# A feed-forward up projection with both halves of the split tokens in one 512-column matmul, and a gate through Silu

## The chip, the cores and the metric

The kernel runs on one core of one Trainium2 chip. The metric is the device time of one execution in microseconds (us), and the kernel before takes 456.35 us (median of 3 runs, 455.64 to 457.35).

## The reference

One layer of a transformer trunk on 256 tokens of width 1024: a sparse-attention mixer, a cross attention to 256 memory tokens, and a convolutional feed-forward block, each behind an RMS norm and added to the residual, with a last RMS norm. Everything is float32. The change sits in the feed-forward block:

```python
def conv_ffn(h, w_up, conv_w, w_down):          # w_up 1024 x 5632, w_down 2816 x 1024
    gate, val = jnp.split(h @ w_up, 2, axis=-1)
    return (jax.nn.silu(causal_dwconv(gate, conv_w)) * val) @ w_down
```

`causal_dwconv` is a causal convolution over the tokens with three taps per channel.

## The kernel before

TensorE multiplies in the type fp32r. To keep float32 accuracy every operand is split into a high part (the value copied to fp32r by ScalarE, `split_hi`, L200, or L122 for weights) and a low part (value minus high part, a subtraction on VectorE, `split_lo`, L204, or L126 for weights). A product is then three matmuls into the same accumulator, `mm3` (L195 to L197): high weight by high token, high weight by low token, low weight by high token. The product of the two low parts is left out.

Weights stream from HBM in half chunks of 128 x 1024 (`load_half`, L114, on SP's queue). Each half is split ahead of its use: ScalarE writes `hi` (L122), VectorE writes `lo` (L126), into six buffers each, so that a split can start only when the matmuls that read the sixth half before it are done. `half` (L129) runs this some four halves ahead of the matmul that asks for the weight (`wtile`, L152).

The feed-forward block works on 22 tiles of 128 gate channels and 128 value channels (`NF`, index `fi`). Its tokens are `h3`, transposed, eight blocks of 128 channels by 256 tokens, high and low part in a tile each. The first three tiles (`ups`, L1095 to L1105) are computed with the tokens as the stationary operand, half of the tokens at a time, copied by ScalarE (`ut`) and transposed back on TensorE into two banks of the tag S and one of O; they start before the second half of the tokens is normed. The other 19 tiles go through `proj_ws` (L290): the weights are stationary, the 256 tokens move, eight steps of three matmuls for the gate (left half of a PSUM bank) and eight for the value (right half). Their banks rotate over the tags PT, proj and S, two banks each.

Behind each tile, ScalarE copies the gate to SBUF (`g`, L1116) and scales it by the last tap (`c`, L1119), VectorE adds the other two taps (L1120, L1121), ScalarE takes the tanh of half the sum (L1123), VectorE forms the gate (L1124) and multiplies it by the value, which it reads from PSUM (`av`, L1126). ScalarE and VectorE then split `av` into `aT_hi` (L200) and `aT_lo` (L204). The down projection (`pd`, L1144 to L1153) reads these, with tokens stationary and 512 or 256 weight columns moving.

SP's and GpSimd's instructions keep the order in which they are written (`manual_schedule`). For TensorE, ScalarE and VectorE a planner fixes the order of the feed-forward block when the program is built, by its own estimate of when operands and buffers are ready. On the chip each engine then runs its list in that order and waits where an operand is late.

Of the kernel before, what the change touches and what calls it, by code (L numbers as in the profile page):

```python
# [10 lines left out]
F32 = mybir.dt.float32  # L11
F32R = mybir.dt.float32r
BF16 = mybir.dt.bfloat16
AF = mybir.ActivationFunctionType
ALU = mybir.AluOpType
AX = mybir.AxisListType

P = 128
D = 1024
S = 256  # L20
NT = S // P
KT = D // P
# [20 lines left out]
def trunk_kernel(ctx: ExitStack, tc: tile.TileContext, a, out):  # L43
    nc = tc.nc
# [4 lines left out]
    act = ctx.enter_context(tc.tile_pool(name="act", bufs=1))  # L49
# [3 lines left out]
    def bank(tag, name):  # L53
        return psum.tile([P, 512], F32, tag=tag, name=name, bufs=2)
# [26 lines left out]
    def add_chunks(name, n, width=2048, start=0):  # L81
        first = len(chunks)
        for i in range(start, start + n):
            chunks.append((a[name][i], width))
        return first
# [66 lines left out]
    def wtile(i, k, c, n):  # L152

        hi, lo = half(i, k // 4, k % 4)
        o = (k % 4) * 256 + c
        return hi[:, o:o + n], lo[:, o:o + n]
# [28 lines left out]
    c_up = add_chunks("w_up", NF)  # L185
# [6 lines left out]
    def mm3(ps, lw, rx, start, stop):  # L192

        (lh, ll), (rh, rl) = lw, rx
        nc.tensor.matmul(ps, lh, rh, start=start, stop=False)  # L195
        nc.tensor.matmul(ps, lh, rl, start=False, stop=False)  # L196
        nc.tensor.matmul(ps, ll, rh, start=False, stop=stop)  # L197
# [85 lines left out]
    def act_pair(nm, tag, pool=act):  # L283
        return tuple(pool.tile([P, KT, S], F32R, tag=f"{tag}_{x}", name=f"{nm}_{x}") for x in ("hi", "lo"))

    def xk(pair, k, t=None):
        s = slice(0, S) if t is None else slice(t * P, (t + 1) * P)
        return pair[0][:, k, s], pair[1][:, k, s]

    def proj_ws(ps, ci, ct, pair, t=None):  # L290

        for k in range(KT):
            mm3(ps, wtile(ci, k, ct * P, P), xk(pair, k, t), k == 0, k == KT - 1)

    def proj_ws_steps(ps, ci, ct, pair):

        for k in range(KT):
            mm3(ps, wtile(ci, k, ct * P, P), xk(pair, k), k == 0, k == KT - 1)
            yield
# [41 lines left out]
    with tc.tile_pool(name="attn", bufs=1, reuse_waits="tile") as at:  # L341
# [9 lines left out]

        hT = act_pair("hT", "aA")

        xT = act.tile([P, KT, S], F32, tag="aB_hi", name="xT")
        rs_x = at.tile([P, NT], F32, name="rs_x")


# [2 lines left out]
        with tc.manual_schedule():  # L360
# [32 lines left out]
            for k0, k1 in PIECES:  # L393
# [3 lines left out]
                if not o:  # L397
                    his.setdefault(c_v + h // 2, []).append(
                        wpool.tile([P, NHALF], F32R, tag="hi", name=f"hi{c_v + h // 2}_{h % 2}", bufs=NBUF))
                    lo = wpool.tile([P, NHALF], F32R, tag="lo", name=f"lo{c_v + h // 2}_{h % 2}", bufs=NBUF)  # L400
                    parts.setdefault(c_v + h // 2, []).append((his[c_v + h // 2][h % 2], lo))
                hi, lo = parts[c_v + h // 2][h % 2]
                cs = slice(o * 512, (o + k1 - k0) * 512)
                split((hi[:, cs], lo[:, cs], v_raw[h][:, cs]))
                for w in range(2):
                    for t in range(NT):
                        for k in ks:
                            rx = (hi, lo)[w][:, (k % 2) * 512:(k % 2 + 1) * 512]
                            for x in range(2 - w):
                                nc.tensor.matmul(pv[t], xk(hT, k, t)[x], rx, start=k == 0 and w == x == 0,  # L410
                                                 stop=k == KT - 1 and w == 1)
# [274 lines left out]
        rs_m = mp.tile([P, NT], F32, name="rs_m")  # L686
        with tc.tile_pool(name="aq", bufs=1, reuse_waits="tile") as aq:

            memT = act_pair("memT", "aB")

            def mem_keys(ci):
                def out(c, ps):
# [303 lines left out]
    with tc.tile_pool(name="cross", bufs=1, reuse_waits="tile") as cr:  # L996
# [46 lines left out]
        def cross_o(h, pT):  # L1043
            po = bank("O", f"xo{h}")
            for dt in range(2):
                col = h * S + dt * P
                for c in range(2):
                    nc.tensor.matmul(po[:, dt * S:(dt + 1) * S], MV[:, c, col:col + P], pT[:, c, :],
                                     start=c == 0, stop=c == 1)
            ks = slice(2 * h, 2 * h + 2)  # L1050
            split((oX[0][:, ks, :], oX[1][:, ks, :], po.rearrange("p (c s) -> p c s", c=2)))
# [6 lines left out]
        for t in range(NT):  # L1058
            for ci in range(EARLY):
                ps = bank("proj", f"pcq{t}{ci}")  # L1060
# [10 lines left out]
        for h in range(4):  # L1071
# [4 lines left out]
                    tick()  # L1076
                tick()
            cross_o(h, pT)
        h3 = act_pair("h3", "aB")
        residual(c_wo, oX, "wo",  # L1080
                 lambda t, sums: norm_t(x_sb[:, t, :], t, h3, C_FFN, f"ffn{t}", "PT", sums),
                 0)
# [4 lines left out]
    with tc.tile_pool(name="ffn", bufs=1, reuse_waits="tile") as fp:  # L1087
        aT = (fp.tile([P, NF, S], F32R, name="aT_hi2"), fp.tile([P, NF, S], F32R, name="aT_lo2"))
        NG = 3
        gbuf = [fp.tile([P, S + 2], F32, name=f"g{i}") for i in range(NG)]  # L1090
        for gb in gbuf:
            nc.gpsimd.memset(gb[:, 0:2], 0.0)

        FIRST = 3
        ups = {fi: bank(("S", "S", "O")[fi], f"up{fi}") for fi in range(FIRST)}  # L1095
        for t in range(NT):
            for fi in range(FIRST):
                ps = bank("proj", f"upt{t}{fi}")
                for k in range(KT):
                    mm3(ps[:, :S], xk(h3, k, t), wtile(c_up + fi, k, 0, S), k == 0, k == KT - 1)  # L1100
                ut = fp.tile([P, S], F32, tag="ut", name=f"ut{t}{fi}", bufs=2)
                nc.scalar.activation(ut, ps[:, :S], AF.Copy)
                for gv_ in range(2):
                    o = gv_ * S + t * P
                    nc.tensor.transpose(ups[fi][:, o:o + P], ut[:, gv_ * P:(gv_ + 1) * P], ident)  # L1105
        wfin = fp.tile([P, D], F32, name="wfin")
        nc.scalar.dma_start(wfin, a["final_w"].to_broadcast([P, D]))
        for fi in range(NF):
            if fi in ups:
                ps = ups.pop(fi)  # L1110
            else:
                ps = bank(("PT", "proj", "S")[fi % 3], f"up{fi}")
                for gv_ in range(2):
                    proj_ws(ps[:, gv_ * S:(gv_ + 1) * S], c_up + fi, gv_, h3)
            gb = gbuf[fi % NG]
            nc.scalar.activation(gb[:, 2:], ps[:, :S], AF.Copy)  # L1116
            c = fp.tile([P, S], F32, tag="c", name=f"c{fi}", bufs=2)
            cw = [cc[:, C_CONV + j * NF + fi:C_CONV + j * NF + fi + 1] for j in range(3)]
            nc.scalar.activation(c, ps[:, :S], AF.Copy, scale=cw[2])  # L1119
            nc.vector.scalar_tensor_tensor(c, gb[:, 1:S + 1], cw[1], c, op0=ALU.mult, op1=ALU.add)  # L1120
            nc.vector.scalar_tensor_tensor(c, gb[:, 0:S], cw[0], c, op0=ALU.mult, op1=ALU.add)  # L1121
            th = fp.tile([P, S], F32, tag="th", name=f"th{fi}", bufs=2)
            nc.scalar.activation(th, c, AF.Tanh, scale=0.5)  # L1123
            nc.vector.scalar_tensor_tensor(c, th, 1.0, c, op0=ALU.add, op1=ALU.mult)  # L1124
            av = fp.tile([P, S], F32, tag="av", name=f"av{fi}", bufs=2)
            nc.vector.scalar_tensor_tensor(av, c, 0.5, ps[:, S:2 * S], op0=ALU.mult, op1=ALU.mult)  # L1126
            split((aT[0][:, fi, :], aT[1][:, fi, :], av))


        H = D // 2  # L1130
        LAST = 6
        ssq = {t: [] for t in range(NT)}
        xw = fp.tile([P, D], F32, name="xw")
        y = [fp.tile([P, D], F32, name=f"y{t}") for t in range(NT)]

        def add_pd(pd, t, h, c0, c1):

            cs = slice(h * H + c0, h * H + c1)
            xs = x_sb[:, t, cs]
            nc.vector.tensor_tensor(xs, pd, xs, op=ALU.add)  # L1140
            ssq[t].append(sumsq(xs, f"f{t}{h}proj"))
            return cs

        for h in range(2):  # L1144

            accs = [(0, 0, H), (1, 0, H)] if h == 0 else [(0, 0, H), (1, 0, H // 2), (1, H // 2, H)]
            pd = [bank((("O", "PT"), ("proj", "proj", "S"))[h][n], f"pd{h}{n}") for n in range(len(accs))]
            plan = [(k, n) for k in range(NF - LAST) for n in range(len(accs))]
            plan += [(k, n) for n in range(len(accs)) for k in range(NF - LAST, NF)]
            for k, n in plan:  # L1150
                t, c, e = accs[n]
                w = wrow(c_dn[h] + k // 4, k % 4)
                mm3(pd[n][:, :e - c], xk(aT, k, t), (w[0][:, c:e], w[1][:, c:e]), k == 0, k == NF - 1)  # L1153
            for n, (t, c, e) in enumerate(accs):
                cs = add_pd(pd[n][:, :e - c], t, h, c, e)
                if t == 1 and n < 2:
                    nc.gpsimd.tensor_tensor(xw[:, cs], x_sb[:, 1, cs], wfin[:, cs], op=ALU.mult)
                elif t == 0 and h == 1:
                    rs = rstd(partial(ssq[0][:1], "f0"), ssq[0][1], "f0")
                    nc.vector.scalar_tensor_tensor(y[0], x_sb[:, 0], rs, wfin, op0=ALU.mult, op1=ALU.mult)  # L1160
                    nc.sync.dma_start(out[0:P, :], y[0])
        t1 = partial(ssq[1][:2], "f1")
        rs = rstd(t1, ssq[1][2], "f1")
        c = 768
        nc.vector.tensor_scalar(y[1][:, :H], xw[:, :H], rs, None, op0=ALU.mult)
        nc.sync.dma_start(out[P:, :H], y[1][:, :H])
        nc.scalar.activation(y[1][:, H:c], xw[:, H:c], AF.Copy, scale=rs)
        nc.vector.scalar_tensor_tensor(y[1][:, c:], x_sb[:, 1, c:], rs, wfin[:, c:], op0=ALU.mult, op1=ALU.mult)
        nc.scalar.dma_start(out[P:, H:], y[1][:, H:])
# [93 lines left out]
```

## Time and profile before

| | |
|---|---|
| median of 3 runs | 456.35 us |
| the profiled execution's own time | 456.24 us |
| its span, first to last instruction | 454.5 us |
| TensorE busy | 443.6 us (98%), 3274 matmuls |
| VectorE busy | 305.6 us (67%) |
| ScalarE busy | 278.8 us (61%) |

The up projection's own matmuls start at 273.4 us of the span, and the down projection takes over at 386.35 us. A busy time here is a union: an instruction whose start lies before the end of the one ahead of it adds only what sticks out. A matmul's listed duration is its time through the array and not what a stream of them pays for each, so costs of matmuls are read from start to start.

### The profile page before, as it was taken

Reading aid. Unit: us, or ns where it says so; the run is one execution under the profiler, and the core shown is the slowest. Engines: PE = TensorE matmul, PEld = TensorE weight load, DVE = VectorE, ACT = ScalarE, POOL = GpSimd, SP = SyncE. Lnnn points to the kernel's source line nnn. Section 1 sums busy time; section 2 is a strip of 40 time slices with the busy share of each in tenths; the row PEclk is TensorE's granted clock in tenths of the full one; section 3 lists DMA queues with packets and bytes.
Section 4 is the critical chain, followed back from the end, with each engine's and each line's share of the span. In section 5 each row is a group of like instructions: output and inputs, shape, how many; then the busy total and the mean of one; then the engine's idle time right before and its main releaser. Section 6 shows DMA issues by size and latency. Waiting matters only on the chain.

```text
span 454.5 us, 8504 instructions
## 1 busy us (share of the span) xinstructions
PE 443.6 (98%) x3274; PEld 406.9 (90%) x3274; DVE 305.6 (67%) x592; ACT 278.8 (61%) x569; POOL 38.7 (9%) x80
## 2 busy tenths in 40 slices
PE   8999999999999999999999999999999999999994
PEld 4999889899988778999988899999999999888984
DVE  4765489779776895756543858878777777745413
ACT  6785496768786886765552757666655556435301
POOL 4240000521200000100000010000000000001003
PEclk9999999999999999999999999999999999999999
DMA  8995958723232005554334537655555555554302
GB/s 295 370 376 186 315 211 273 220 95 112 94 94 94 1 1 191 180 182 147 118 107 143 179 104 238 222 187 187 184 187 184 184 185 183 186 191 154 127 0 94
DMA packets 22073, 77.04 MB, mean 170 GB/s; under 512 B 2576, under 2 KB 3088, under 8 KB 22032
## 3 DMA queue, kind: packets, MB, share of 16 engines
q1 hardware_dynamic: 21312, 74.39, 48.5%
q10 hardware_dynamic: 720, 2.10, 1.2%
q8 instruction: 26, 0.43, 0.4%
q14 instruction: 15, 0.12, 0.1%
HBM read 75.43 MB, written 1.05 MB: 168 GB/s over the span
## 4 chain that ended last, share of the span: by engine, by line
PE 84%; ACT 5%; DMA 4%; DVE 2%; issue 2%; POOL 1%; SPq 0%; POOLq 0%; DVEq 0%; ACTq 0%
PE up L195 8%; PE up L197 8%; PE up L196 8%; PE pd L196 5%; PE pd L197 5%; PE pd L195 5%; PE pt L852 2%; PE O L876 2%; PE pmk L197 2%; PE pmk L195 2%; PE pcq L195 2%; PE pmk L196 2%; PE pcq L196 2%; PE pmv L196 2%; PE pmv L195 2%; PE pmv L197 2%
## 5 line engine op out<-in xcount | busy, mean ns | idle before, releaser
L126 DVE TENSOR_TENSOR lo<-raw,hi 128x1024 fp32r<-128x1024 f32 x122 | 148.7, 1223 | 69.5 <-ACT hi L122 68.7
L122 ACT ACTIVATE hi<-raw 128x1024 fp32r<-128x1024 f32 x122 | 128.6, 1059 | 59.3 <-PE pd L197 17.7
L195 PE MATMUL up<-h_hi,hi 128*128 128x256 f32 x304 | 86.1, 283 | 0.0
L196 PE MATMUL up<-h_lo,hi 128*128 128x256 f32 x304 | 86.0, 283 | 0.0
L197 PE MATMUL up<-h_hi,lo 128*128 128x256 f32 x304 | 86.0, 283 | 0.0
L196 PEld LDWEIGHTS up<-h_lo,hi 128*128 128x128 f32 x304 | 58.4, 192 | 0.0
L197 PEld LDWEIGHTS up<-h_hi,lo 128*128 128x128 f32 x304 | 58.4, 192 | 0.0
L195 PEld LDWEIGHTS up<-h_hi,hi 128*128 128x128 f32 x304 | 58.4, 192 | 0.0
L197 PE MATMUL pd<-hi,aT_lo 128*128 128x512 f32 (+1 forms) x110 | 38.4, 349 | 0.0
L196 PE MATMUL pd<-lo,aT_hi 128*128 128x512 f32 (+1 forms) x110 | 38.4, 349 | 0.0
L195 PE MATMUL pd<-hi,aT_hi 128*128 128x512 f32 (+1 forms) x110 | 38.4, 349 | 0.0
L828 ACT ACTIVATE pp<-pp,nm 128x128 f32<-128x128 f32 (+1 forms) x64 | 28.4, 446 | 7.6 <-DVE nm L821 7.6
L821 DVE CUSTOM_DVE_ANT_0 pp<-s,tri,nrs 128x128 f32<-128x128 f32 (+1 forms) x64 | 23.4, 412 | 6.5 <-PE s L809 4.1
L196 PEld LDWEIGHTS pd<-lo,aT_hi 128*128 128x128 f32 x110 | 20.7, 188 | 2.9
L195 PEld LDWEIGHTS pd<-hi,aT_hi 128*128 128x128 f32 x110 | 20.7, 188 | 2.9
L197 PEld LDWEIGHTS pd<-hi,aT_lo 128*128 128x128 f32 x110 | 20.7, 188 | 2.9
L1123 ACT ACTIVATE th<-c 128x256 f32<-128x256 f32 x22 | 9.1, 414 | 22.2 <-DVE c L1121 22.2
L195 PE MATMUL pq<-hT_hi,hi 128*128 128x256 f32 x64 | 18.5, 289 | 0.4 <-ACT hi L122 0.4
L196 PE MATMUL pmv<-lo,memT_hi 128*128 128x256 f32 x64 | 18.5, 289 | 0.0
L195 PE MATMUL pmv<-hi,memT_hi 128*128 128x256 f32 x64 | 18.5, 288 | 0.0
L197 PE MATMUL pmk<-memT_hi,lo 128*128 128x256 f32 x64 | 18.3, 286 | 0.0
L197 PE MATMUL pq<-hT_hi,lo 128*128 128x256 f32 x64 | 18.3, 288 | 0.0
(295 smaller groups left out, 1096.5 us busy)
## 6 DMA issues: line engine op xcount, KB each, us to landing
raw<-in_w_up SPq DMA_DIRECT2D x44, 512.0 KB, 4.3
raw<-in_w_dn SPq DMA_DIRECT2D x20, 512.0 KB, 4.6
raw<-in_w_q SPq DMA_DIRECT2D x8, 512.0 KB, 6.1
raw<-in_w_mk SPq DMA_DIRECT2D x8, 512.0 KB, 5.0
raw<-in_w_mv SPq DMA_DIRECT2D x8, 512.0 KB, 4.0
raw<-in_w_out SPq DMA_DIRECT2D x8, 512.0 KB, 3.8
raw<-in_ca_wq SPq DMA_DIRECT2D x8, 512.0 KB, 4.3
raw<-in_ca_wo SPq DMA_DIRECT2D x8, 512.0 KB, 4.2
```

Source lines behind the costliest of these rows:

```text
L122: nc.scalar.activation(his[i][h], raws[i][h], AF.Copy)
L126: nc.vector.tensor_tensor(t, raws[i][h], f(his[i][h]), op=ALU.subtract)
L195: nc.tensor.matmul(ps, lh, rh, start=start, stop=False)
L196: nc.tensor.matmul(ps, lh, rl, start=False, stop=False)
L197: nc.tensor.matmul(ps, ll, rh, start=False, stop=stop)
L821: nc.vector.tensor_tensor_reduce(self.p[br], self.s[:, br * w:(br + 1) * w], tri[:, 1 - t:].rearrange("p h k -> p (h k)"), nrs[:, t:t + 1] ...
L828: nc.scalar.activation(self.p[br], self.p[br], AF.Exp, bias=pair.nm[:, j, br:br + 1], scale=-1.0, accum_out=pair.den[:, j, br:br + 1])
L852: nc.tensor.transpose(self.pt[n][:, o * P:(o + 1) * P], self.pp[:, j, br, h * P:(h + 1) * P], ident)
L876: nc.tensor.matmul(O[j * DK:(j + 1) * DK, pair.m * P:(pair.m + 1) * P], V[:, h, br, g, :], pair.block(j, br, h), start=False, stop=(br, h) ...
L1123: nc.scalar.activation(th, c, AF.Tanh, scale=0.5)
```

## The change

A new `act_both` puts the high and the low part of the tokens into one tile, for each block of channels 256 high columns and then 256 low ones. A new `proj_wide` replaces `proj_ws` for the 19 tiles: for each step the high weight meets all 512 columns in one matmul into a whole bank, and the low weight meets the 256 high columns, added into the left half of that bank. So the bank holds two sums that have still to be added, and the gate and the value have a bank each. The banks rotate over four tags, PT with proj for even tiles and S with O for odd ones.

On the way out ScalarE copies the left half to SBUF and VectorE adds the right half, for the gate into `g` and for the value into a new tile `vb`. The scaling by the last tap reads `g` instead of PSUM. Silu takes the place of the tanh and of the instruction that formed the gate from it, for all 22 tiles. The tile that held the transposed input and the memory's tokens ahead of `h3` takes the new shape too.

```diff
+    def act_both(nm):
+        both = act.tile([P, 2 * KT, S], F32R, tag="aB", name=nm).rearrange("p (k b) s -> p k b s", b=2)
+        return (both[:, :, 0], both[:, :, 1]), both
+
+    def proj_wide(ps, ci, ct, both):
+        for k in range(KT):
+            hi, lo = wtile(ci, k, ct * P, P)
+            nc.tensor.matmul(ps, hi, both[:, k], start=k == 0, stop=False, skip_group_check=True)
+            nc.tensor.matmul(ps[:, :S], lo, both[:, k, 0], start=False, stop=k == KT - 1, skip_group_check=True)
...
-        xT = act.tile([P, KT, S], F32, tag="aB_hi", name="xT")
+        xT = act.tile([P, 2 * KT, S], F32, tag="aB", name="xT")[:, :KT]
...
-            memT = act_pair("memT", "aB")
+            memT, _ = act_both("memT")
...
-        h3 = act_pair("h3", "aB")
+        h3, x3 = act_both("h3")
...
             if fi in ups:
                 ps = ups.pop(fi)
             else:
-                ps = bank(("PT", "proj", "S")[fi % 3], f"up{fi}")
+                wide = [bank(("PT", "proj", "S", "O")[(2 * fi + gv_) % 4], f"up{fi}{gv_}") for gv_ in range(2)]
                 for gv_ in range(2):
-                    proj_ws(ps[:, gv_ * S:(gv_ + 1) * S], c_up + fi, gv_, h3)
+                    proj_wide(wide[gv_], c_up + fi, gv_, x3)
+                ps = None
             gb = gbuf[fi % NG]
-            nc.scalar.activation(gb[:, 2:], ps[:, :S], AF.Copy)
             c = fp.tile([P, S], F32, tag="c", name=f"c{fi}", bufs=2)
             cw = [cc[:, C_CONV + j * NF + fi:C_CONV + j * NF + fi + 1] for j in range(3)]
-            nc.scalar.activation(c, ps[:, :S], AF.Copy, scale=cw[2])
+            if ps is None:
+                nc.scalar.activation(gb[:, 2:], wide[0][:, :S], AF.Copy)
+                nc.vector.tensor_tensor(gb[:, 2:], wide[0][:, S:], gb[:, 2:], op=ALU.add)
+                vb = fp.tile([P, S], F32, tag="vb", name=f"vb{fi}", bufs=2)
+                nc.scalar.activation(vb, wide[1][:, :S], AF.Copy)
+                nc.vector.tensor_tensor(vb, wide[1][:, S:], vb, op=ALU.add)
+            else:
+                nc.scalar.activation(gb[:, 2:], ps[:, :S], AF.Copy)
+                vb = ps[:, S:2 * S]
+            nc.scalar.activation(c, gb[:, 2:], AF.Copy, scale=cw[2])
             nc.vector.scalar_tensor_tensor(c, gb[:, 1:S + 1], cw[1], c, op0=ALU.mult, op1=ALU.add)
             nc.vector.scalar_tensor_tensor(c, gb[:, 0:S], cw[0], c, op0=ALU.mult, op1=ALU.add)
             th = fp.tile([P, S], F32, tag="th", name=f"th{fi}", bufs=2)
-            nc.scalar.activation(th, c, AF.Tanh, scale=0.5)
-            nc.vector.scalar_tensor_tensor(c, th, 1.0, c, op0=ALU.add, op1=ALU.mult)
+            nc.scalar.activation(th, c, AF.Silu)
             av = fp.tile([P, S], F32, tag="av", name=f"av{fi}", bufs=2)
-            nc.vector.scalar_tensor_tensor(av, c, 0.5, ps[:, S:2 * S], op0=ALU.mult, op1=ALU.mult)
+            nc.vector.tensor_tensor(av, th, vb, op=ALU.mult)
             split((aT[0][:, fi, :], aT[1][:, fi, :], av))
```

## Rows read from the trace of the kernel before

**Rows 1.** The page: busy time of each engine, share of the span, instructions
```profile
PE 443.6 (98%) x3274; PEld 406.9 (90%) x3274; DVE 305.6 (67%) x592; ACT 278.8 (61%) x569; POOL 38.7 (9%) x80
```

**Rows 2.** Busy time by stage: stretch, length, PE, PEld, DVE, ACT, POOL, TensorE clock
```profile
273.40:291.00 17.60, 17.60 (x150) 17.60 (x149) 15.34 (x24) 12.71 (x25) 0.00 (x0) 1.00 0.72 232
315.00:387.00 72.00, 72.00 (x599) 71.91 (x599) 55.05 (x88) 44.10 (x76) 0.00 (x0) 1.00 0.55 185
```

**Rows 3.** Waits, 273 to 386 us: who waited for whom: total, times, longest
```profile
ACT th L1123 <- DVE c L1121: 22.2, 14, 1.7
DVE lo L126 <- ACT hi L122: 13.2, 20, 1.5
ACT hi L122 <- PE up L196: 11.8, 21, 1.6
DVE c L1124 <- ACT th L1123: 7.3, 14, 0.5
```

**Rows 4.** Timeline of PE in the up projection: start, duration, line, operation
```profile
282.60 0.36 PE L195 MATMUL up<-h_hi,hi 128*128 128x256 f32 x1
...
291.07 0.28 PE L196 MATMUL up<-h_lo,hi 128*128 128x256 f32 x1
291.19 0.28 PE L197 MATMUL up<-h_hi,lo 128*128 128x256 f32 x1
...
386.35 0.39 PE L195 MATMUL pd<-hi,aT_hi 128*128 128x512 f32 x1
```

**Rows 5.** Timeline of PE in the down projection, where widths 512 and 256 alternate
```profile
417.49 0.39 PE L197 MATMUL pd<-hi,aT_lo 128*128 128x512 f32 x1
417.72 0.28 PE L195 MATMUL pd<-hi,aT_hi 128*128 128x256 f32 x1
...
418.31 0.28 PE L197 MATMUL pd<-hi,aT_lo 128*128 128x256 f32 x1
418.43 0.39 PE L195 MATMUL pd<-hi,aT_hi 128*128 128x512 f32 x1
...
419.13 0.28 PE L195 MATMUL pd<-hi,aT_hi 128*128 128x256 f32 x1
```

**Rows 6.** Groups by line, DVE and ACT: shapes, count, busy, mean ns, idle before
```profile
L1124 DVE SCALAR_TENSOR_TENSOR c<-th,c 128x256 f32<-128x256 f32 x22 | 9.3, 423 | 7.3 <-ACT th L1123 7.3
L1126 DVE SCALAR_TENSOR_TENSOR av<-c,up 128x256 f32<-128x256 f32 x22 | 9.2, 419 | 0.6
L1119 ACT ACTIVATE c<-up,cc 128x256 f32<-128x256 f32 x22 | 10.3, 468 | 0.0
L1123 ACT ACTIVATE th<-c 128x256 f32<-128x256 f32 x22 | 9.1, 414 | 22.2 <-DVE c L1121 22.2
L1116 ACT ACTIVATE g<-up 128x256 f32<-128x256 f32 x22 | 8.0, 369 | 2.1 <-PE up L1105 2.1
L389 ACT ACT_TABLE_LOAD x1 | 1.3, 1283 | 1.2 <-PEq L1255 1.2
```

**Rows 7.** Timeline of DVE behind one tile: starts closer together than their durations
```profile
308.05 0.42 DVE L1126 SCALAR_TENSOR_TENSOR av<-c,up 128x256 f32<-128x256 f32 x1
308.39 0.48 DVE L1120 SCALAR_TENSOR_TENSOR c<-g,cc,c 128x256 f32<-128x256 f32 x1
```

**Rows 8.** Timeline of the block's head: first wide tile, first tile's chain
```profile
273.40 0.28 PE L195 MATMUL up<-h_hi,hi 128*128 128x256 f32 x1
276.04 0.38 PE L1105 MATMUL up<-ident,ut 128*128 128x128 f32 x2
276.45 0.39 ACT L1116 ACTIVATE g<-up 128x256 f32<-128x256 f32 x1 [1.52 <-PE up L1105]
279.23 0.28 PE L197 MATMUL upt<-hi,h_lo 128*128 128x256 f32 x1
282.14 0.41 DVE L1126 SCALAR_TENSOR_TENSOR av<-c,up 128x256 f32<-128x256 f32 x1
```

## The prediction

> **What bounds the kernel now.** I read the busy shares first: TensorE is busy 98% of the span, VectorE 67%, ScalarE 61% [rows 1]. An average can hide a stage with another limit, so the table by stage comes next. In the up projection TensorE is busy 72.00 of 72.00 us at a granted clock of 1.00 (its upper level, 2.4 GHz), VectorE 55.05 and ScalarE 44.10 [rows 2]. The waits say the same from the other side: ScalarE's weight copies wait for matmuls to free a buffer, 11.8 us in 21 waits [rows 3]. The weights are thus split as early as the six buffers allow. TensorE sets the pace, and what the change is worth is read first from the spacing of the matmuls, then from whether the other two engines still keep up.
>
> **TensorE.** Tiles 4 to 21 run from 282.60 to 386.35 us: 18 tiles of 48 matmuls, 864 in 103.75 us, 0.1201 us from start to start for 256 columns [rows 4]. A step of three costs 0.360 us. For 512 columns the down projection gives the price: from 386.35 to 417.72 us it issues 135 such matmuls (22 rows of channels x 2 halves of the tokens x 3, and three more), 31.37 us, 0.2324 us each [rows 4, 5]. A new step is one of each, 0.3525 us. The saving is 0.0077 us a step, and over 19 tiles x 16 steps = 304 steps 2.3 us. The second half of the down projection has the two widths beside each other: six of 256 columns take 0.71 us (417.72 to 418.43), three of 512 take 0.70 us (418.43 to 419.13) [rows 5]. One of each is then 0.3517 us, a saving of 0.0085 us, 2.6 us in all. The steps between the widths are not dearer: 0.23 us from a 512 to the 256 after it, 0.12 us the other way [rows 5]. So the columns stay the same, 768 a step, and what goes is the fixed part of one matmul in three. I take 2.5 us, between the two readings. It can't be much more: 2 x 0.1201 - 0.2324 = 0.0078 us is all that two narrow matmuls pay above a wide one, and the mixed stretch, with 2 x 0.1183 - 0.2333 = 0.0033 us at its own narrow price, shows that this difference is small and uncertain, so an end near 1.0 us (304 x 0.0033) belongs to the range. No row shows widths that change with every matmul; a wide one that hides the next weight load better could bring the narrow one to the 0.1183 us of the mixed stretch with the wide one at 0.2324, 0.3507 us a step, 2.9 us.
>
> The Trainium skill ("TensorE: Matmul & The Clock Gate", section "Back-to-back issue gap") puts the spacing at full clock at the columns over 2.4 plus 2.5 ns, whatever the width. By it a dropped matmul gives back 2.5 ns, 304 x 2.5 ns = 0.8 us. The rows speak against its size, since 0.1201 us lies 13 ns above 256 columns and 0.2324 us 19 ns above 512.
>
> **VectorE.** In the steady stretch it is busy 55.05 / 72.00 = 76% [rows 2], which is 4.41 us of a tile's period of 48 x 0.1201 = 5.76 us. Each of the 19 tiles loses the instruction that formed the gate (L1124, 423 ns) and gains two additions that read PSUM. No row has just these; the nearest is `av`, which reads PSUM too, 419 ns [rows 6], or 0.34 us where the next one starts into its end [rows 7]. The net is +0.34 to +0.42 us; I take the upper end, 4.83 us. The new period is 16 x 0.352 = 5.63 us. So VectorE goes from 76% to 86%, and the time in which it may wait falls from 1.35 to 0.80 us a tile. Cost at the end of the kernel: none, as TensorE still covers it. If that cover is gone, every 0.1 us by which VectorE's work and waits pass 5.63 us is 1.9 us over the 19 tiles.
>
> **ScalarE.** It is busy 44.10 / 72.00 of the period, 3.53 us. It gains the copy of the value, like `g` 369 ns, and the scaling reads SBUF where it read PSUM, at most its own 468 ns and, by its neighbours, no less than 369 [rows 6]. The sum is about 3.9 of 5.63 us, 69%. Silu for tanh is one ACTIVATE of the same shape; I price it at the tanh's 414 ns, and from the 369 of a copy to the 468 of the scaled copy it moves the sum by 0.05 us. A table load takes 1283 ns and the trace has one, at the very start [rows 6]. Another function may need another one: between none and two, 0 to 2.6 us on ScalarE once, behind 2.1 us a tile that it has free. I take one, at no cost to TensorE.
>
> **New waits and buffers.** The scaling by the last tap now waits for VectorE's addition where it followed the copy at once. Behind it on ScalarE stand the weight copies (L122), for which VectorE's subtraction (L126) waits, and for that the matmuls. A half lasts 24 matmuls, 2.9 us, and with six buffers one comes free five halves, some 14 us, before the half split into it is used: a split that starts a few us late is still early. The PSUM banks give four tiles of room instead of six, yet each is free after its two readers and not after the whole chain. At the start of the down projection its banks come from tiles 18 and 19, long read.
>
> **The head.** Before, the first wide tile (3) used a bank of PT and started at 273.40 us, while the first three tiles were still on their way: its matmuls filled TensorE between their pieces until 279.23 us and beyond [rows 8]. Now its gate needs the bank of S that tile 0 holds, until that tile's `av` has read the value. That took until 282.14 us, 5.7 us after its `g` at 276.45 us [rows 8], and a table load may lie in it. Tile 3's value half (a bank of O) and tile 4 (PT and proj) need no such bank: 8 x 0.352 = 2.8 us and 5.6 us of other work. With them in place it costs nothing; that is what I take. Without them TensorE would wait the length of the chain less the pieces still to do, 282.14 - 279.23 = 2.9 us, and with the load 4.2 us.
>
> **Sum.** The profiled execution took 456.24 us with a span of 454.5 us; what lies outside the span is not touched. 456.24 - 2.5 = 453.7 us, and the median of the runs shown is 0.1 us above that execution: 453.8 us.
>
> **The rivals.**
> *The head eats the gain.* For it: the planner orders by its own estimates, and the S bank is a true new dependence. Against: other matmuls are there to fill. With 1.5 to 4.2 us lost the net is -1.0 to +1.7 us, 455.4 to 458.1 us; about 456.5 us.
> *Two narrow matmuls cost hardly more than a wide one.* By the mixed stretch's own difference, 1.0 us saved: 455.3 us. The page's fixed cost would land beside it, at 455.6 us.
> *VectorE becomes the bound; slower.* Its in-order list now changes hands with ScalarE once more a tile (copy, addition, scaling), and in the steady stretch it already waits 13.2 us for weight copies and 7.3 us for the tanh [rows 3]. If its 1.35 us of waiting a tile does not shrink, the period is 4.83 + 1.35 = 6.18 us, 0.42 us longer than today's 5.76, and 19 tiles make +8.0 us: 464.3 us. It decides once the waits stay over 0.93 us a tile; at 1.1 us it is +0.17 x 19 = 3.2 us, 459.6 us. Against it: these waits hang on weight copies which themselves wait for TensorE, so they vanish when VectorE is late; and in the head, from 273.40 to 291.00 us, VectorE is busy 15.34 of 17.60 us, 87%, and TensorE all of it [rows 2].
> *The change doesn't do what it says.* The planner lays out the whole program anew, the tile shared with the input and memory's tokens included, and another stage shifts by 1 to 2 us either way: 452 to 456 us.
>
> **How the numbers follow.** The forecast holds 0.47 (452.9 to 454.7 us by itself), the head 0.19, the small difference 0.10, VectorE 0.18, the new layout 0.06. A measurement can tell about 0.5%, 2.3 us, from no change, which puts "faster" below 454.07 us. The forecast lies just beyond that line: 0.36 of its 0.47 counts as faster, with 0.03 of the layout, and 0.01 of the head, 0.40. Slower, over 458.6 us, are 0.16 of VectorE, 0.03 of the head and 0.01 of the layout, 0.20. The rest, 0.40, is no change. The range goes from 452.6 us, the largest saving (2.9 us) with a little of the layout, to 459.6 us, VectorE's rival at 1.1 us of waits; beyond lies about half of that rival and little below.
>
> **What would show it.** Right: pairs of starts 0.23 and 0.12 us apart in the up projection, its tiles 5.6 us apart, TensorE busy throughout, VectorE near 86%, weight copies still waiting for matmuls. Wrong: matmuls that wait for `lo` or for an addition in the steady stretch (VectorE), gaps on TensorE between 266 and 285 us that end with `av` of tile 0 (the head), pairs 0.36 us apart (no fixed part saved), or a second table load in front of a matmul that waits.

## The result, and the profile after

The changed kernel takes 452.38 us (median of 6 runs, 451.78 to 452.71) beside 456.99 us of the kernel before in the same session; the ratio is 0.9899, with an interval of 0.9881 to 0.9918. It is faster by 4.6 us where 2.5 us were forecast, and lies 0.2 us below the low end of the range.

The page of the changed kernel: busy time of each engine, its share of the span, instructions.

```profile
PE 439.4 (98%) x2970; PEld 390.4 (87%) x2970; DVE 306.6 (68%) x608; ACT 285.5 (63%) x589; POOL 38.8 (9%) x80
```

Against [rows 1] there are 304 matmuls fewer, one for each step, and the share of the weight loads (PEld) falls from 90% to 87%. Busy TensorE time is down by 4.2 us. The table by stage of the changed kernel, columns as in [rows 2]:

```profile
273.40:291.00 17.60, 17.60 (x112) 15.80 (x111) 14.24 (x22) 15.02 (x29) 0.00 (x0) 1.00 0.64 208
315.00:381.00 66.00, 66.00 (x383) 58.29 (x382) 53.84 (x96) 44.29 (x85) 0.00 (x0) 1.00 0.60 189
```

In the steady stretch TensorE is still never idle. What is new is the second pair of numbers: weight loads cover 58.29 of 66.00 us, where they covered 71.91 of 72.00 before [rows 2]. VectorE is at 53.84 / 66.00 = 82%, not 86%. The timeline of TensorE in that stretch (start, duration, line, operation), and the handover to the down projection:

```profile
345.71 0.28 PE L307 MATMUL up<-h,lo 128*128 128x256 f32 x1
345.83 0.39 PE L306 MATMUL up<-h,hi 128*128 128x512 f32 x1
346.06 0.28 PE L307 MATMUL up<-h,lo 128*128 128x256 f32 x1
346.18 0.39 PE L306 MATMUL up<-h,hi 128*128 128x512 f32 x1
...
381.88 0.39 PE L195 MATMUL pd<-hi,aT_hi 128*128 128x512 f32 x1
```

Read from start to start, a wide matmul takes 0.23 us and a narrow one 0.12. Over the 265 pairs between 290 us and the handover the means are 0.2300 and 0.1167 us, a step of 0.3467 us. Before, every start in the same stretch lay 0.1200 us behind the one ahead, a step of 0.3600 us (0.3602 by [rows 4], whose first step is a little longer). That is 0.0133 us a step, 4.1 us over 304 steps.

From the first matmul of the feed-forward block to the first of the down projection it was 128.88 us before (257.47 to 386.35) and is 124.97 us now (256.91 to 381.88): 3.91 us less. The down projection and the tail last as long as before. The other 0.56 us of the two profiled executions lies ahead of the block, and it is no part of the change: the same early matmul of the input's norm (`pb_x`) starts at 25.61 us in the kernel before and 24.89 in the changed one, but also at 24.92 in the third experiment below, whose code up to there is that of the kernel before, and at 26.39 in the first, whose code there is that of the changed one. So what lies ahead of the block varies from execution to execution by more than that.

The waits of the changed kernel between 273 and 381 us, columns as in [rows 3]:

```profile
ACT g L1134 <- PE up L307: 18.4, 16, 1.3
DVE lo L126 <- ACT hi L122: 15.2, 16, 1.1
ACT hi L122 <- PE up L306: 9.3, 18, 0.9
DVE vb L1138 <- ACT vb L1137: 1.1, 1, 1.1
```

ScalarE waits for matmuls, and VectorE for ScalarE's weight copies, which wait for matmuls themselves; TensorE waits for nothing. The additions cost no wait of note (one, at the head). The waits for the tanh, 7.3 us in [rows 3], are gone. The groups of the new operations (line, shapes, count, busy, mean ns, idle before):

```profile
L1135 DVE TENSOR_TENSOR g<-up,g 128x256 f32<-128x256 f32 x19 | 7.9, 416 | 0.0
L1138 DVE TENSOR_TENSOR vb<-up,vb 128x256 f32<-128x256 f32 x19 | 7.9, 418 | 1.1 <-ACT vb L1137 1.1
L1137 ACT ACTIVATE vb<-up 128x256 f32<-128x256 f32 x19 | 6.9, 362 | 1.7 <-PE up L307 1.7
L1142 ACT ACTIVATE c<-g,cc 128x256 f32<-128x256 f32 x22 | 10.8, 496 | 0.1
L1146 ACT ACTIVATE th<-c 128x256 f32<-128x256 f32 x22 | 9.1, 413 | 0.3 <-DVE c L1144 0.3
```

The additions take 416 and 418 ns, priced at 419. Silu takes 413 ns, as the tanh did (414). The scaling takes 496 ns from SBUF, more than from PSUM (468), where I had put 468 as the upper end.

The head of the block in the changed kernel, timelines of TensorE, ScalarE and VectorE, as in [rows 8]:

```profile
272.84 0.40 PE L306 MATMUL up<-h,hi 128*128 128x512 f32 x1
276.08 0.38 ACT L1137 ACTIVATE vb<-up 128x256 f32<-128x256 f32 x1 [1.72 <-PE up L307]
279.07 0.28 PE L197 MATMUL upt<-hi,h 128*128 128x256 f32 x1
279.43 1.28 ACT L1146 ACT_TABLE_LOAD   x1
281.17 0.42 DVE L1148 TENSOR_TENSOR av<-th,up 128x256 f32<-128x256 f32 x1 [0.51 <-ACT th L1146]
```

The first copy on the way out is a value (`vb`), not a gate: the planner drew the value half of tile 3 ahead, into the free bank of O, while the gate's bank of S was held by tile 0 until the `av` at 281.17 us. Between 273.40 and 291.00 us TensorE is not idle for a moment, table load included.

### The profile page after: what moved, and what is told of

It is laid out like the page before. It is cut to its first block, busy times and chain, and to the rows that moved or that the text cites. A ratio compares the mean times of both kernels' runs of the same rounds, so it can differ in the third digit from the quotient of the medians.

```text
span 450.0 us, 7928 instructions
## 1 busy us (share of the span) xinstructions
PE 439.4 (98%) x2970; PEld 390.4 (87%) x2970; DVE 306.6 (68%) x608; ACT 285.5 (63%) x589; POOL 38.8 (9%) x80
## 4 chain that ended last, share of the span: by engine, by line
PE 84%; DMA 5%; ACT 4%; DVE 2%; issue 2%; POOL 1%; SPq 1%; POOLq 0%; DVEq 0%; ACTq 0%
PE up L306 15%; PE up L307 8%; PE pd L195 5%; PE pd L196 5%; PE pd L197 5%; DMA raw<-in_w_q 3%; PE pt L866 2%; PE O L890 2%; PE pmk L197 2%; PE pmk L195 2%; PE pcq L195 2%; PE pmk L196 2%; PE pcq L196 2%; PE pmv L196 2%; PE pmv L195 2%; PE pmv L197 2%
## 5 line engine op out<-in xcount | busy, mean ns | idle before, releaser
L306 PE MATMUL up<-h,hi 128*128 128x512 f32 x304 | 105.5, 392 | 0.0
L307 PE MATMUL up<-h,lo 128*128 128x256 f32 x304 | 85.5, 281 | 0.0
L306 PEld LDWEIGHTS up<-h,hi 128*128 128x128 f32 x304 | 56.9, 187 | 12.3
L307 PEld LDWEIGHTS up<-h,lo 128*128 128x128 f32 x304 | 57.7, 190 | 0.1
L1134 ACT ACTIVATE g<-up 128x256 f32<-128x256 f32 x19 | 7.3, 382 | 18.4 <-PE up L307 18.4
L196 PE MATMUL pmv<-lo,memT 128*128 128x256 f32 x64 | 18.5, 290 | 0.0
L195 PE MATMUL pmv<-hi,memT 128*128 128x256 f32 x64 | 18.5, 289 | 0.0
L197 PE MATMUL pmk<-memT,lo 128*128 128x256 f32 x64 | 18.3, 286 | 0.0
L195 PE MATMUL pmk<-memT,hi 128*128 128x256 f32 x64 | 18.2, 285 | 0.0
L196 PE MATMUL pmk<-memT,hi 128*128 128x256 f32 x64 | 18.2, 284 | 0.0
```

The costliest lines, as they stand in the source:

```text
L306: nc.tensor.matmul(ps, hi, both[:, k], start=k == 0, stop=False, skip_group_check=True)
L307: nc.tensor.matmul(ps[:, :S], lo, both[:, k, 0], start=False, stop=k == KT - 1, skip_group_check=True)
L1134: nc.scalar.activation(gb[:, 2:], wide[0][:, :S], AF.Copy)
```

## The experiments

The gain came from TensorE's matmuls, as forecast, but not in the size forecast, so the question was why a step costs 0.3467 us and not 0.3525. Theory N: a stream of narrow matmuls is paced at 0.120 us by the weight load that goes with each, not by its 256 columns, and a wide matmul hides the load that follows it. Its rivals: the layout or the banks (L), a fixed cost for each matmul whatever its neighbours (F), the rate at which instructions are issued (I). A second question was how much cover TensorE has left for VectorE, and a third whether the same pair of widths pays elsewhere.

The changed kernel's own trace already limits theory N. Two of its weight loads, beside the matmuls of 345.49 to 345.83 us:

```profile
345.49 0.19 PEld L307 LDWEIGHTS up<-h,lo 128*128 128x128 f32 x1
345.72 0.19 PEld L306 LDWEIGHTS up<-h,hi 128*128 128x128 f32 x1
```

Every load starts about 3 ns behind a matmul and belongs to the next one. Behind a wide matmul it is over, by its listed 0.19 us, before the next start. Behind a narrow one it is not, yet the wide matmul starts after 0.1167 us, with the same load of 128 columns in between as in the stream that goes at 0.1200. So a fixed 0.120 us for each load can't be the whole account; a load that is held up by the one ahead of it, where that isn't over, would fit, but no run shows it by itself.

**The width alone.** The wide matmul becomes two narrow ones; everything else of the change stays. (Written so, the kernel's sums lack a part, the first step's product of the two high parts as far as can be told. The matmuls, their shapes and their order are those wanted.)

```diff
-            nc.tensor.matmul(ps, hi, both[:, k], start=k == 0, stop=False, skip_group_check=True)
+            nc.tensor.matmul(ps[:, :S], hi, both[:, k, 0], start=k == 0, stop=False, skip_group_check=True)
+            nc.tensor.matmul(ps[:, S:], hi, both[:, k, 1], start=k == 0, stop=k == KT - 1, skip_group_check=True)
```

> The changed kernel with its one 512-column matmul split into two of 256 columns (high tokens, then low tokens, each with its own weight load); layout, banks, additions on the way out and Silu all stay. Theory N (a stream of narrow matmuls is paced at 0.120 us by the weight load that goes with each, and a wide one hides the load that follows it): the step goes back to 3 x 0.120 = 0.360 us from 0.3467, 304 steps x 0.0133 = 4.0 us more than the changed kernel, 456.0 to 456.8 us, ratio to the kernel before 0.998 to 1.000. Rival L (the gain comes from the tile that holds both parts side by side, or from a bank of its own for gate and value): the step stays near 0.347 us and the time at about 452.4 us.

Measured: 457.14 us, ratio to the kernel before 1.0002 (0.9985 to 1.0018). Timeline of its TensorE:

```profile
345.34 0.28 PE L306 MATMUL up<-h,hi 128*128 128x256 f32 x1
345.46 0.28 PE L307 MATMUL up<-h,hi 128*128 128x256 f32 x1
345.58 0.28 PE L308 MATMUL up<-h,lo 128*128 128x256 f32 x1
345.70 0.28 PE L306 MATMUL up<-h,hi 128*128 128x256 f32 x1
```

The step is 0.36 us again, the block lasts 128.89 us (258.57 to 387.46) as before, and the whole gain is gone, with the layout, the banks, the additions and Silu all in place. L falls. This is also the price of all those parts together: nothing beyond the interval of some 0.8 us.

**Narrower still.** The low weight's matmul in two of 128 columns.

```diff
-            nc.tensor.matmul(ps[:, :S], lo, both[:, k, 0], start=False, stop=k == KT - 1, skip_group_check=True)
+            for o in (0, P):
+                nc.tensor.matmul(ps[:, o:o + P], lo, both[:, k, 0, o:o + P], start=False, stop=k == KT - 1, skip_group_check=True)
```

> The changed kernel with the 256-column matmul of the low weight split into two of 128 columns, each with its own weight load. Theory N: a narrow matmul can't be followed before about 0.11 to 0.12 us however few columns it has, so the two take 0.22 to 0.24 us where one took 0.117: the step is 0.45 to 0.47 us and the kernel 304 x 0.11 = 33 us longer, about 485 us. Rival F (each matmul costs its columns, 0.45 ns each, and a fixed part of 2 to 8 ns whatever its neighbours): two of 0.060 to 0.066 us, a step of 0.35 to 0.36 us, 1 to 3 us longer, about 454 us.

Measured: 488.07 us (one run). Timeline of its TensorE, the two halves in one line:

```profile
345.53 0.45 PE L306 MATMUL up<-h,hi 128*128 128x512 f32 x1
345.82 0.33 PE L308 MATMUL up<-h,lo 128*128 128x128 f32 x2
345.99 0.45 PE L306 MATMUL up<-h,hi 128*128 128x512 f32 x1
```

The columns are the same, and a step takes 0.46 us. The block, 260.00 to 418.14 us, is 33.2 us longer, 0.109 us a step for one more load and matmul. F, which gave 1 to 3 us, falls: half the columns buy almost nothing. N has the total right but not its parts. The second half starts 0.058 us behind the first, where N allowed no matmul within 0.11 us of another, and the first half starts 0.287 us behind the wide one (means of 280 steps). Nor does this run tell N from I: beside the two halves, loads and matmuls start in turn 0.05 to 0.06 us apart, and at that rate of issue a load and a matmul would cost 0.11 us too.

**Which part of the pair.** In the kernel before, the six middle steps of each projection load and use 96 of the 128 weight columns, so that the last 32 channels of a tile lack these six steps.

```diff
-            mm3(ps, wtile(ci, k, ct * P, P), xk(pair, k, t), k == 0, k == KT - 1)
+            n = P if k in (0, KT - 1) or ci < c_up else 96
+            mm3(ps[:n], wtile(ci, k, ct * P, n), xk(pair, k, t), k == 0, k == KT - 1)
```

> The kernel before, with only 96 of the 128 weight columns of each up-projection tile loaded and multiplied in the six middle steps of eight (its output leaves that part of the product out). The 256 moving columns and the number of instructions stay. Theory N: a shorter weight load lets the narrow stream go at the pace of its columns, 0.117 us in the middle steps instead of 0.120: 38 x 6 x 3 = 684 matmuls x 0.003 = 2.1 to 2.3 us less, about 454 us. Rival I (the pace is that of issuing two instructions, a load and a matmul, 60 ns each): 0.120 us stays, time as before, 456 to 457 us.

Measured: 453.32 us (one run). Timeline of its TensorE, 11 starts from the first line to the last:

```profile
345.28 0.27 PE L195 MATMUL up<-h_hi,hi 128*96 128x256 f32 x1
345.39 0.28 PE L196 MATMUL up<-h_lo,hi 128*96 128x256 f32 x1
...
346.55 0.28 PE L197 MATMUL up<-h_hi,lo 128*96 128x256 f32 x1
```

The busy times of 60 us of it, columns as in [rows 2]:

```profile
315.00:375.00 60.00, 60.00 (x516) 60.00 (x515) 47.97 (x76) 37.75 (x65) 0.00 (x0) 1.00 0.56 185
```

With a quarter fewer weight columns and the same 256 moving columns, the stream goes at 1.27 / 11 = 0.1155 us in place of 0.1200; over the 565 such pairs between 290 us and the handover the mean is 0.1159. The block is 126.18 us (257.25 to 383.43), 2.7 us less than before, out of 2.9 us between the two profiled executions. The number of instructions is unchanged, so I falls as what sets the 0.1200. The pace depends on the number of weight columns. That it is the load is not shown, since the matmul works with 96 columns too, and a quarter fewer columns saved only 3% of the time. At the seams the order is even against N: behind a matmul of 96, with a load of 128 in between, the next starts after 0.117 us (34 cases), and behind a matmul of 128, with a load of 96 in between, after 0.120 us (33 cases).

**The order alone.** Four wide matmuls in a row, then the four narrow ones of the same weights.

```diff
-        for k in range(KT):
...
+        for j in range(0, KT, 4):
+            for k in range(j, j + 4):
+                hi, lo = wtile(ci, k, ct * P, P)
+                nc.tensor.matmul(ps, hi, both[:, k], start=k == 0, stop=False, skip_group_check=True)
+            for k in range(j, j + 4):
+                hi, lo = wtile(ci, k, ct * P, P)
+                nc.tensor.matmul(ps[:, :S], lo, both[:, k, 0], start=False, stop=k == KT - 1, skip_group_check=True)
```

> The changed kernel with four wide matmuls in a row and then the four narrow ones of the same weights, in place of one after the other. Same matmuls, same columns. Theory N: a narrow one that follows a narrow one is paced at 0.120 us again; three of each four do, 38 x 8 x 0.75 = 228 x 0.0034 = 0.8 us more than the changed kernel, about 453.2 us, and in the trace narrow to narrow 0.120 and narrow to wide 0.117 us. Rival F: every narrow one 0.117 us as in the changed kernel, time the same, 452.4 us.

Measured: 453.50 us (453.17 to 454.05), ratio to the kernel before 0.9921 (0.9906 to 0.9936). Timeline of its TensorE, four in a line:

```profile
330.85 0.63 PE L310 MATMUL up<-h,lo 128*128 128x256 f32 x4
331.32 1.09 PE L307 MATMUL up<-h,hi 128*128 128x512 f32 x4
332.25 0.64 PE L310 MATMUL up<-h,lo 128*128 128x256 f32 x4
332.73 1.09 PE L307 MATMUL up<-h,hi 128*128 128x512 f32 x4
```

Four narrow ones take 0.47 to 0.48 us, 0.1185 us each over 67 such runs; N asks for one at 0.117 and three at 0.120, 0.1192 on the mean, and F for 0.1167. F, by which neighbours don't matter, falls here too. N's placing fails as well: narrow to narrow is 0.1186 us and narrow to wide 0.1183, where it had 0.120 and 0.117, and the shortest of the four is the one right behind a wide matmul (0.1174). And four wide ones take 0.93 us, 0.2323 each, where a wide one between narrow ones takes 0.2300, and that was in neither theory. Together the step is 0.3508 us and the block 126.10 us (257.15 to 383.25), 1.1 us longer than in the changed kernel, whose block lasts 124.97 and 124.98 us in its two profiled executions. So the alternation itself is worth 1 us in the block. The medians alone would not show it: 453.50 us lies 1.1 us above the changed kernel's first median and 0.5 above its second (453.03, below), and the intervals of the ratios overlap. How a step divides between its two matmuls is less firm than its sum: in the kernel with the tanh, next, it reads 0.2317 and 0.1150 us, again 0.3467 together.

**Silu, and VectorE's cover.** The tanh and its extra instruction come back; then, in two kernels, two and four more additions a tile that nobody reads.

```diff
-            nc.scalar.activation(th, c, AF.Silu)
+            nc.scalar.activation(th, c, AF.Tanh, scale=0.5)
+            nc.vector.scalar_tensor_tensor(c, th, 1.0, c, op0=ALU.add, op1=ALU.mult)
```

```diff
+                for _ in range(2):
+                    idle = fp.tile([P, S], F32, tag="idle", name=f"idle{fi}{_}", bufs=2)
+                    nc.vector.tensor_tensor(idle, vb, vb, op=ALU.add)
```

> The changed kernel with the gate through tanh and its extra VectorE instruction again, the wide matmuls kept. In the steady stretch VectorE goes from 4.53 us a tile (53.84 / 66.00 of 5.55) by 0.34 to 0.42 to 4.87 to 4.95 of 5.55 us. Theory C (VectorE's work alone has to fit the period, its waits vanish when it is late): hidden, 452.0 to 452.8 us, so that Silu's share of the gain is nothing by itself. Rival W (its waits of 1.02 us a tile stay): a period of 5.89 to 5.97 us, 19 x 0.38 = 7 us longer, about 459.5 us.

> The changed kernel with two additions per wide tile whose result nobody reads, on VectorE: 0.68 to 0.84 us more a tile, 5.21 to 5.37 of 5.55 us. Theory C: still hidden, 452.4 to 453 us. Rival W: 13 to 16 us longer, 465 to 468 us.

> The changed kernel with four such additions: 5.89 to 6.21 us of VectorE work a tile, over the 5.55 us of TensorE. Theory C: VectorE sets the pace and the matmuls wait for weights, 19 x 0.34 to 0.66 = 6.5 to 12.5 us longer less what the six buffered halves absorb, 457 to 465 us. Rival W: 26 to 32 us longer, 478 to 484 us.

Measured: 452.90 us (ratio 0.9915, 0.9892 to 0.9938) with the tanh, 452.89 us (0.9904, 0.9879 to 0.9930) with two additions, 454.85 us (0.9952, 0.9935 to 0.9968) with four. The same 60 us by stage of the three, one fence each, DVE being the third pair:

```profile
315.00:375.00 60.00, 60.00 (x348) 52.48 (x347) 53.89 (x102) 41.45 (x79) 0.00 (x0) 1.00 0.56 191
```

```profile
315.00:375.00 60.00, 60.00 (x347) 52.88 (x346) 56.65 (x111) 41.68 (x79) 0.00 (x0) 1.00 0.56 189
```

```profile
315.00:375.00 60.00, 60.00 (x345) 52.37 (x344) 57.12 (x119) 38.10 (x69) 0.00 (x0) 1.00 0.54 182
```

At 90% and at 94% of VectorE the block lasts 125.01 and 124.98 us, as long as in the changed kernel (124.97): work that fits the period is free, and the waits shrink to make room. VectorE's longest wait in the block, 15.2 us in the changed kernel, with the tanh and with two additions (273 to 386 us):

```profile
DVE lo L126 <- ACT hi L122: 10.5, 16, 1.1
DVE lo L126 <- ACT hi L122: 6.2, 15, 0.8
```

W falls. Silu saves an instruction that was covered anyway. At four additions the profiled execution is 2.1 us longer from the start of the block to the last matmul of the down projection, less than the 6.5 to 12.5 us that I expected, and 454.85 us lies under the expected 457 to 465. The planner had drawn down-projection matmuls ahead (the first starts at 376.59 us, the last of the up projection at 386.30), and TensorE was busy with these. It waits once, in the down projection and for VectorE's chain. Two starts lie 1.70 us apart there, where 0.23 us is usual, and that is most of the 2.1 us:

```profile
391.53 0.40 PE L197 MATMUL pd<-hi,aT_lo 128*128 128x512 f32 x1
393.23 0.47 PE L195 MATMUL pd<-hi,aT_hi 128*128 128x512 f32 x1 [1.30 <-DVE vb L1138]
```

So VectorE begins to cost time between two and four additions, and little at first.

**The same pair elsewhere.** The memory's keys through a wide and a narrow matmul (64 steps), then the cross attention's queries too (48 steps), each with a copy and an addition on the way out. They ran beside the changed kernel.

```diff
-                    nc.vector.tensor_tensor(mT[:, c], ps[:, :S], row_m, op=ALU.mult)
+                    nc.scalar.activation(mT[:, c], ps[:, :S], AF.Copy)
+                    nc.vector.tensor_tensor(mT[:, c], ps[:, S:], mT[:, c], op=ALU.add)
+                    nc.vector.tensor_tensor(mT[:, c], mT[:, c], row_m, op=ALU.mult)
...
-                    yield from proj_ws_steps(ps[:, :S], c_mk + ci, ct, memT)
+                    yield from proj_wide_steps(ps, c_mk + ci, ct, memB)
```

> The changed kernel once more, beside the two below on the same chip: about 452.4 us, ratio to the kernel before 0.990.

> The changed kernel with the keys of the memory (eight blocks of 128 channels, 64 steps) through the same pair of a wide and a narrow matmul, one ScalarE copy and one VectorE addition more a block. Theory N with TensorE as the bound of that stage: 64 x 0.0133 = 0.85 us less than the changed kernel, 451.5 us. Rival (that stage waits for the heads of the attention, whose work on ScalarE and VectorE the additions delay): no less, 452.4 us, or up to 1 us more.

> The same and the queries of the cross attention too (three of four, 48 steps; a copy and an addition for each of six blocks, which the split of the queries now waits for). Theory N: another 48 x 0.0133 = 0.64 us, 450.9 us. Rival: the chain from the queries to their scores gets longer by a copy and an addition, 0.8 us for each of three heads, and TensorE has too little beside it: up to 2.4 us more, 453 us.

Measured: 453.03 us for the changed kernel (ratio to the kernel before 0.9909, 0.9892 to 0.9926), 454.55 us with the keys (0.9955, 0.9940 to 0.9970), 455.12 us with the queries too (0.9970, 0.9955 to 0.9984). Both are slower than the changed kernel. The stage of the attention heads by busy time, first in the changed kernel (the run beside them), then with the keys:

```profile
110.00:150.00 40.00, 39.81 (x346) 36.41 (x345) 31.86 (x103) 29.65 (x90) 3.68 (x3) 1.00 0.32 105
150.00:187.00 37.00, 35.96 (x261) 29.34 (x260) 29.12 (x83) 28.74 (x79) 0.98 (x3) 1.00 0.22 73
```

```profile
110.00:150.00 40.00, 38.44 (x327) 34.23 (x326) 33.42 (x116) 30.58 (x98) 0.73 (x1) 1.00 0.23 80
150.00:187.00 37.00, 35.40 (x251) 28.30 (x251) 28.45 (x85) 28.84 (x82) 0.98 (x3) 1.00 0.22 72
```

TensorE is idle for 1.2 us of these 77 with the pair in the up projection alone, and for 3.2 us with the keys as well. The keys' matmuls stand there to fill TensorE while the heads wait for ScalarE and VectorE. Two reasons fit, and they were not separated: shorter fillers leave it idle sooner, and the additions put work on the engines that the heads wait for. No version beat the changed kernel.

## Why the prediction was right or wrong

- **What bounds the kernel: right.** TensorE was never idle in the up projection before or after, and the change was worth what its matmuls saved.
- **TensorE's saving: the step that failed, by size.** I wrote that "a new step is one of each", a wide matmul at 0.2324 us and a narrow one at 0.1201 us, 0.3525 us, or 0.3517 us from the mixed stretch. It measured 0.2300 and 0.1167, 0.3467 us: 4.1 us where I took 2.5, and beyond my end of 2.9, past which I wrote that "It can't be much more". Both prices came from rows in which a matmul has neighbours of its own width, and the price depends on the neighbours: the same two matmuls cost 0.3508 us a step in runs of four and 0.3467 in turn. The mixed stretch has runs of three and six [rows 5], in which most of the difference is gone; I had priced something close to the kernel with runs of four. The block saved 3.91 us in place of 2.5, and that 1.4 us is about the whole distance from the forecast of 453.8 us to the 452.38 us measured. Why a narrow matmul costs less beside a wide one stays open: that a weight load paces it is argued from the 96 weight columns (0.1159 us in place of 0.1200) and not shown.
- **"So the columns stay the same, 768 a step, and what goes is the fixed part of one matmul in three": only half right.** A fixed part for each matmul explains neither the run with two matmuls of 128 columns nor the one with another order. The table by stage held a hint, weight loads busy for 71.91 of 72.00 us [rows 2], which I didn't use. It is no proof: loads listed at 0.19 us and started every 0.12 us always overlap, and the share is full with 96 weight columns too, 60.00 of 60.00 us at a quicker pace.
- **The Trainium skill's formula** ("TensorE: Matmul & The Clock Gate", section "Back-to-back issue gap"), as I used it, gave 2.5 ns a matmul and 0.8 us in all: the saving of 4.1 us is five times that. The section gives this formula for a matmul by itself, which I left out. It also says that in a stream of weight loads and matmuls both set the spacing, and the run with 96 weight columns agrees as far as it goes: 0.1159 in place of 0.1200 us, with fewer weight columns in load and matmul alike.
- **VectorE: right that it is covered; the load was put too high**, 86% against 82%. The work a tile rose by about 0.12 us and not by 0.34 to 0.42, since a busy time is a union and the instructions without waits between them overlap. The durations by themselves rose by 0.47 us a tile (57.97 us in 72.00 before, 60.82 in 66.00 now), and the overlap took 0.35 of that. The rival in which VectorE's waits do not shrink was refuted at 90% and 94%.
- **ScalarE and the table load: right.** Silu as long as the tanh, one load of 1283 ns, no cost.
- **The head: right.** The value half of tile 3 filled TensorE, as forecast, and it cost 0.2 us at most: 4.1 us of steps less the 3.91 us of the block.
- **The rest** of the 4.6 us between the medians, 0.7 us, is variation: in the last session the changed kernel's median was 453.03 us beside 456.90, 3.87 us less, as much as the block saves.

## What to carry to other kernels

Price a matmul from a stream with the same neighbours as it will have: a narrow one with its own weight load, put beside a wide one, saved more here than the count of matmuls and a fixed price for each would give. Where no row has those neighbours, say so in the range and leave it open at that end. A covered engine's waits are not a cost to carry over, as they gave way to work up to 94% of the period. The same edit in a stage where the matmuls are filler for a chain on other engines lost time.

## What the runs showed of the hardware that was not expected

The same matmuls cost more or less by what stands beside them, at the same granted clock of 1.00: one of 512 and one of 256 columns, each with its own weight load, take 0.3467 us in turn and 0.3508 us in runs of four. The cause stays open. A matmul of 128 columns with its own weight load added 0.109 us to the step, nearly as much as one of 256 costs (0.1167). ScalarE's copy with a scale was slower from SBUF (496 ns) than from PSUM (468 ns) for the same 128 x 256. Silu brought one table load of 1283 ns, and the ACTIVATE behind it started as it ended (279.43 and 280.72 us).
